# Winograd block sums of the down projection's data, made in the up projections instead of in the down projections

## The chip, the cores and the metric

One core of one Trainium2 chip. The metric is device time in microseconds of one execution; the kernel before takes 2208.18 us, the median of 3 runs (2207.48 to 2209.02).

## The reference

Two layers on a sequence of 1024 tokens of width 1024, float32. Layer 0 mixes tokens with a chunked gMLP, layer 1 with differential attention; each is followed by the gated MLP with a causal depthwise convolution, which is where the change lies. Around each sub-layer stand RMS norms and a residual.

```python
def conv_ffn(x, w_up, conv_w, conv_b, w_down):          # w_up: 1024 x 5632, w_down: 2816 x 1024
    h = causal_dwconv(x @ w_up, conv_w, conv_b)         # 3 taps
    g, u = h[..., :D_FF], h[..., D_FF:]                 # D_FF = 2816 = 22 x 128
    return (jax.nn.gelu(g) * u) @ w_down
...
    h = h + rmsnorm(y, norm_g[layer, 1])
    y = rmsnorm(h, norm_g[layer, 2])
    y = conv_ffn(y, ffn_w_up[layer], ffn_conv_w[layer], ffn_conv_b[layer], ffn_w_down[layer])
    h = h + rmsnorm(y, norm_g[layer, 3])
```

## The kernel before

**Precision.** Every float32 product is made of three passes of a reduced float type: `split` (line 168) rounds an operand on ScalarE (line 170, `hi`) and takes the rest on VectorE (line 173, `lo`); the passes are hi x hi, hi x lo, lo x hi. So each operand tile costs one ScalarE cast and one VectorE subtraction before TensorE (line 162) can use it.

**Seven products for eight.** Large products are cut into 2 x 2 blocks and made by Winograd's form of Strassen's scheme: seven block products, with sums of blocks of both operands before and of the results after.

**Up projections** (`ffn`, from line 1081): a loop over 22 features j of 128 columns, each with its gate and its value column block, so 22 pairs and in each 7 products of 12 matmuls. The weights of a pair are loaded on SyncE, GpSimd makes four sums of them (lines 983, 986, 987, 991), they are split; `Winograd.rest` (line 1060) runs the products and collects them on ScalarE (line 1025) and VectorE (line 1029). Then `convolve(j)` works on the pair's two columns: ScalarE scales one (line 1092), VectorE adds two taps (line 1094), the same for the other, ScalarE applies gelu (line 1098), VectorE multiplies (line 1099), and the product, 128 features x 1024 tokens, is stored on the DRAM tensor `pd` in two halves of 512 tokens (line 1101). From j = 4 on, GpSimd also makes block sums of the down projection's weights (`weight_sum`, lines 400 to 403, stored on `td` in line 405).

**Down projections** (`down`, line 421). The data operand A is 2816 features x 1024 tokens: A11 and A12 are the first half of the tokens with features 0 to 10 and 11 to 21, A21 and A22 the second half. `load` (line 432) brings a whole block, 11 features, into three tiles `t8` of 8 KB per partition; there are 15 such tiles in all. `combine` (line 444) makes the block sums in place on GpSimd: six instructions each (five of two features, 1024 elements, one of one), four sums: S1 = A21 + A22, S2 = S1 - A11, S3 = A22 - S2 (equal to A11 - A21), S4 = A12 - S2. `product` makes one block product of 132 matmuls: six pairs (k, n) of features; `operands` splits the data pair x and the weight pair w (raw weights in 4 tiles `wr`, split ones in 7 tiles `w4`); the last `tail` pairs are run row block by row block, so that results come out one by one. The order is A11 B11, A22 T4, A12 B21, S2 T2, S1 T1, S4 B22, S3 T3. For the results of the last two, `end` (line 328) adds norm and residual (lines 337, 343, 306 on VectorE) and stores.

**What sets the order.** The Tile layer puts the instructions of each engine into one in-order queue when the program is built, by its own model of when each can run, so an instruction may stand elsewhere than in the code. Every engine runs its queue in order; a waiting instruction holds all behind it. All DMAs stand on SyncE's queue, the loads into `wr` and `t8` among them, which wait there until a tile is free.

## Time and profile before

| | us |
|---|---|
| median of 3 runs (lowest, highest) | 2208.18 (2207.48, 2209.02) |
| profiled execution | 2211.13 |
| its span | 2209.4 |
| TensorE busy | 2132.1 (97%) |
| VectorE busy | 1697.2 (77%) |
| ScalarE busy | 1089.0 (49%) |
| GpSimd busy | 892.2 (40%) |

The mean granted clock of TensorE is 0.988 of full speed. In the profile PE is TensorE, PEld its weight loads, DVE VectorE, ACT ScalarE, POOL GpSimd, SPq SyncE's queue. A row names the line, the engine, the operation and the tiles that it writes and reads, without their numbers. The up projections run from about 340 to 760 us in layer 0 and from 1540 to 1980 in layer 1, each followed by a down projection to about 970 us and to the end. Busy shares over the whole span hide stages with different limits, so stretches are read one by one.

### The profile page before, as it was taken

Reading aid. Unit: us, or ns where it says so; the run is one execution under the profiler, and the core shown is the slowest. Engines: PE = TensorE matmul, PEld = TensorE weight load, DVE = VectorE, ACT = ScalarE, POOL = GpSimd, SP = SyncE. Lnnn points to the kernel's source line nnn. Section 1 sums busy time; section 2 is a strip of 40 time slices with the busy share of each in tenths; the row PEclk is TensorE's granted clock in tenths of the full one; section 3 lists DMA queues with packets and bytes.
Section 4 is the critical chain, followed back from the end, with each engine's and each line's share of the span. In section 5 each row is a group of like instructions: output and inputs, shape, how many; then the busy total and the mean of one; then the engine's idle time right before and its main releaser. Section 6 shows DMA issues by size and latency. Waiting matters only on the chain.

```text
span 2209.4 us, 27390 instructions
## 1 busy us (share of the span) xinstructions
PE 2132.1 (97%) x10072; PEld 1736.2 (79%) x10072; DVE 1697.2 (77%) x1967; ACT 1089.0 (49%) x1914; POOL 892.2 (40%) x751
## 2 busy tenths in 40 slices
PE   8979998999999998999999999999899999999998
PEld 6868786888888877887777777778688888887787
DVE  6654659878888788588588888866988888878856
ACT  5322435545455544465356665654545555554443
POOL 1264126666657084143000101222565666618512
PEclk9989999999999999999999999999999999999999
DMA  6232422544444562354411110233244444456224
GB/s 238 86 124 92 162 86 74 195 143 150 155 162 149 203 225 90 110 183 132 155 34 53 49 49 20 86 134 124 69 135 161 161 148 158 160 187 235 86 96 167
DMA packets 156647, 288.63 MB, mean 131 GB/s; under 512 B 11360, under 2 KB 75744, under 8 KB 156512
## 3 DMA queue, kind: packets, MB, share of 16 engines
q1 hardware_dynamic: 156512, 286.88, 37.9%
q8 instruction: 79, 1.29, 0.2%
q14 instruction: 56, 0.46, 0.1%
HBM read 210.29 MB, written 76.55 MB: 130 GB/s over the span
## 4 chain that ended last, share of the span: by engine, by line
PE 81%; DVE 10%; ACT 3%; DMA 2%; POOL 2%; issue 2%; SPq 0%; DVEq 0%; POOLq 0%; ACTq 0%
PE ps L162 77%; DVE t L173 2%; PE pst L162 2%; DVE w L173 2%; PE pst L843 1%; ACT e L824 1%; PE pst L296 1%; DVE t L1094 1%; DVE cols L1029 0%; DVE xs L306 0%; DVE e L830 0%; DMA wr<-in_b_wv 0%; DVE h L343 0%; DMA wr<-td 0%; DVE sm L821 0%
## 5 line engine op out<-in xcount | busy, mean ns | idle before, releaser
L162 PE MATMUL ps<-t,w 128*128 128x512 f32 x4848 | 1150.3, 394 | 16.2 <-ACT tm L1025 7.3
L162 PEld LDWEIGHTS ps<-t,w 128*128 128x128 f32 x4848 | 900.5, 189 | 215.6 <-ACT tm L1025 9.9
L162 PE MATMUL ps<-w,t 128*128 128x512 f32 x2512 | 602.4, 396 | 18.8 <-DVE t L173 12.6
L162 PEld LDWEIGHTS ps<-w,t 128*128 128x128 f32 x2512 | 472.7, 190 | 122.3 <-DVE t L173 16.5
L173 DVE TENSOR_TENSOR w<-wr,w 128x512 fp32r<-128x512 f32 (+1 forms) x266 | 334.4, 1263 | 160.8 <-ACT w L170 71.0
L170 ACT CAST w<-wr 128x512 fp32r<-128x512 f32 (+1 forms) x268 | 218.5, 821 | 212.7 <-PE ps L162 207.5
L1094 DVE SCALAR_TENSOR_TENSOR t<-cols,cw,t 128x1023 f32<-128x1023 f32 (+1 forms) x176 | 260.7, 1481 | 19.0 <-ACT t L1092 17.1
L173 DVE TENSOR_TENSOR t<-t,t 128x1024 fp32r<-128x1024 f32 (+1 forms) x124 | 185.2, 1525 | 16.2 <-ACT t L170 16.2
L446 POOL TENSOR_TENSOR t<-t,t 128x1024 f32<-128x1024 f32 (+1 forms) x48 | 147.2, 3103 | 115.9 <-PE ps L162 114.6
L173 DVE TENSOR_TENSOR w<-wt,w 128x512 fp32r<-128x512 f32 x176 | 169.6, 974 | 18.2 <-ACT w L170 18.1
L1025 ACT COPY tm<-ps 128x512 f32<-128x512 f32 x136 | 79.0, 581 | 150.8 <-PE ps L162 150.8
L170 ACT CAST t<-t 128x1024 fp32r<-128x1024 f32 (+1 forms) x124 | 105.6, 888 | 79.1 <-PE ps L162 57.8
L983 POOL TENSOR_TENSOR wt<-wr,wr 128x512 f32<-128x512 f32 x44 | 66.5, 1512 | 192.4 <-DMA wr<-in_ffn_up 128.5
L1092 ACT ACTIVATE t<-cols,cw 128x1024 f32<-128x1024 f32 x88 | 109.7, 1247 | 57.4 <-DVE cols L1029 57.2
L162 PE MATMUL ps<-t,t 64*128 64x512 f32 (+4 forms) x792 | 129.2, 376 | 0.8 <-ACT e L824 0.4
L202 POOL TENSOR_SCALAR sm<-sm 128x1 f32<-128x1 f32 (+1 forms) x48 | 15.4, 322 | 265.7 <-ACT ot L863 161.1
L338 POOL TENSOR_SCALAR sm<-sm 128x1 f32<-128x1 f32 x32 | 22.3, 698 | 245.0 <-ACT y L336 244.7
L170 ACT CAST w<-wt 128x512 fp32r<-128x512 f32 x176 | 108.2, 622 | 22.5 <-PE ps L162 15.5
L162 PEld LDWEIGHTS ps<-t,t 64*128 64x128 f32 (+1 forms) x792 | 91.2, 188 | 34.3 <-issue 11.1
L824 ACT ACTIVATE e<-ps,sm 128x128 f32<-128x128 f32 (+7 forms) x128 | 94.2, 745 | 28.8 <-DVE sm L816 22.7
L173 POOL TENSOR_TENSOR t<-wr,t 128x1024 fp32r<-128x1024 f32 (+1 forms) x16 | 36.4, 2281 | 171.1 <-ACT t L170 171.1
L1029 DVE TENSOR_TENSOR cols<-ps,tm 128x512 f32<-128x512 f32 x132 | 90.0, 682 | 18.1 <-PE ps L162 16.4
(155 smaller groups left out, 2453.4 us busy)
## 6 DMA issues: line engine op xcount, KB each, us to landing
wr<-in_ffn_up SPq DMA_DIRECT2D x88, 512.0 KB, 4.0
wr<-in_ffn_down SPq DMA_DIRECT2D x94, 256.0 KB, 3.4
pd<-t SPq DMA_DIRECT2D x88, 256.0 KB, 2.6
td<-wr SPq DMA_DIRECT2D x88, 256.0 KB, 2.5
wr<-td SPq DMA_DIRECT2D x40, 512.0 KB, 3.7
t<-pd SPq DMA_DIRECT2D x16, 1024.0 KB, 8.1
wr<-in_ffn_down SPq DMA_DIRECT2D x30, 512.0 KB, 3.6
hd<-h SPq DMA_DIRECT2D x24, 512.0 KB, 2.6
```

The lines of the kernel that those rows point to most:

```text
L162: nc.tensor.matmul(o, a, b, start=first, stop=last, skip_group_check=onto)
L170: i = nc.scalar.copy(hi, src)
L173: return (engine or nc.vector).tensor_tensor(lo, src, hi.bitcast(F32), ALU.subtract)
L296: nc.tensor.transpose(pt[:, k * P:(k + 1) * P], xs[:, f:f + P], ident)
L338: nc.gpsimd.tensor_scalar(ss, sq[:, 0:1], sq[:, 1:2], EPS, ALU.add, ALU.add)
L446: nc.gpsimd.tensor_tensor(of(o, k, n), of(a, k, n), of(b, k, n), op)
L824: nc.scalar.activation(e[:, :L], si[i], AF.Exp, bias=negm[:, i:i + 1], accum_out=sm[:, i:i + 1])
L983: i = nc.gpsimd.tensor_tensor(t1, b12, b11, ALU.subtract)
L1025: nc.scalar.copy(t, o)
L1029: nc.vector.tensor_tensor(o, a, b, ALU.add)
L1092: nc.scalar.activation(tt, src, AF.Identity, bias=c[:, 3:4], scale=c[:, 2:3])
L1094: nc.vector.scalar_tensor_tensor(tt[:, tap:], src[:, :S - tap], c[:, 2 - tap:3 - tap], tt[:, tap:], ALU.mult, ALU.add)
```

## The change

The features are taken in the order 0, 11, 1, 12, and so on (`feature`), so that an even and the following odd j hold feature k of A11, A21 and feature k of A12, A22. An even j multiplies into a tile `t8` that is kept until the odd one is done, and stores A11. An odd j stores A12 and A22; then GpSimd makes S3, S1, S2 and S4 of 512 elements each in the kept tile and each is stored. `pd` now holds seven blocks of 11 features. In `down`, `load`, `of` and `combine` are gone, and `operands` loads each data pair itself (line 432 after the change) into its own tile, 512 KB a load.

```diff
@@ -427,27 +427,10 @@
         nk = NFF // 2
         pairs = [(k, min(2, nk - k)) for k in range(0, nk, 2)]
         weights = weight_blocks(io["ffn_down"][l], td[l])
-        raw = {}
-
-        def load(a):
-            half, j = int(a[1]) - 1, (int(a[2]) - 1) * nk
-            raw[a] = []
-            for k in range(0, nk, 4):
-                n = min(4, nk - k)
-                t = t8(F32, (P, 4, 512))
-                nc.sync.dma_start(t[:, :n], pd[l][half, j + k:j + k + n].rearrange("j p c -> p j c"))
-                raw[a].append(t)
-
-        def of(a, k, n):
-            return raw[a][k // 4][:, k % 4:k % 4 + n]
-
-        def combine(o, a, b, op):
-            for k, n in pairs:
-                nc.gpsimd.tensor_tensor(of(o, k, n), of(a, k, n), of(b, k, n), op)
-
         def operands(a, b, k, n, apart=False):
-            x = t8(F32R, (P, 2, 2, 512))
-            split(x[:, 0, :n], x[:, 1, :n], of(a, k, n))
+            x, r = t8(F32R, (P, 2, 2, 512)), t8(F32, (P, 4, 512))[:, :n]
+            nc.sync.dma_start(r, pd[l][PARTS.index(a), k:k + n].rearrange("j p c -> p j c"))
+            split(x[:, 0, :n], x[:, 1, :n], r)
             raw = raw_w(weights[b](k, n).rearrange("k p c -> p k c"), n, 512)
             if apart:
                 t = t8(F32R, (P, 2, 2, 512))
@@ -457,7 +440,7 @@
             split(*w, raw)
             return x, w
 
-        def product(a, b, ahead=(), first=None, at=3, tail=SHORT_TAIL, wide=0):
+        def product(a, b, ahead=(), tail=SHORT_TAIL, wide=0):
 
             out = [bank1() for _ in range(4)]
 
@@ -473,8 +456,6 @@
                 xw = ahead[m] if m < len(ahead) else operands(a, b, k, n)
                 for i in range(4):
                     part(i, k, n, *xw)
-                if m == at and first:
-                    first()
             xws = [operands(a, b, k, n, m >= tail - wide) for m, (k, n) in enumerate(pairs[-tail:])]
             for i in range(4):
                 for (k, n), xw in zip(pairs[-tail:], xws):
@@ -482,42 +463,36 @@
                 yield i, out[i]
 
         add = nc.vector.tensor_tensor
-        load("A11")
         ahead = [operands("A11", "B11", *pairs[0])]
         yield
         with tc.tile_pool(name=nm("out"), bufs=1) as pool:
             u2, c11, v = (pool.tile([P, 4, 512], F32, tag=n, name=nm(n)) for n in ("u2", "c11", "v"))
-            for i, r in product("A11", "B11", ahead, lambda: load("A22")):
+            for i, r in product("A11", "B11", ahead):
                 nc.scalar.copy(u2[:, i], r)
             gp = load_g(pool, g_post)
             gn = load_g(pool, g_pre) if g_pre is not None else None
-            load("A21")
-            for i, r in product("A22", "T4", (), lambda: load("A12"), 1):
+            for i, r in product("A22", "T4"):
                 nc.scalar.copy(v[:, i], r)
-
-            combine("A21", "A21", "A22", ALU.add)
-            combine("A11", "A21", "A11", ALU.subtract)
-            combine("A22", "A22", "A11", ALU.subtract)
             for i, r in product("A12", "B21"):
                 add(c11[:, i], r, u2[:, i], ALU.add)
-            combine("A12", "A12", "A11", ALU.subtract)
-            for i, r in product("A11", "T2"):
+            for i, r in product("S2", "T2"):
                 add(u2[:, i], r, u2[:, i], ALU.add)
                 nc.gpsimd.tensor_tensor(v[:, i], v[:, i], u2[:, i], ALU.add)
             u4 = t8(F32, (P, 4, 512))
-            for i, r in product("A21", "T1"):
+            for i, r in product("S1", "T1"):
                 add(u4[:, i], r, u2[:, i], ALU.add)
-            for i, r in product("A12", "B22"):
+            for i, r in product("S4", "B22"):
                 c12 = pool.tile([P, 512], F32, tag="c12", name=nm("c12"), bufs=2)
                 add(c12, r, u4[:, i], ALU.add)
                 end(pool, i, (c11[:, i], c12), h_in, h_out, gp, gn, y_next, n=2)
-            for i, r in product("A22", "T3", tail=TAIL, wide=WIDE):
+            for i, r in product("S3", "T3", tail=TAIL, wide=WIDE):
                 add(v[:, i], r, v[:, i], ALU.add)
                 add(u4[:, i], r, u4[:, i], ALU.add)
                 end(pool, 4 + i, (v[:, i], u4[:, i]), h_in, h_out, gp, gn, y_next, n=2)
 
     hd = [dpool.tile([S, D], F32, name=f"hd{i}", tag=f"hd{i}") for i in range(3)]
-    pd = [dpool.tile([2, NFF, P, 512], F32, name=f"pd{i}", tag=f"pd{i}") for i in range(2)]
+    PARTS = ("A11", "A12", "A22", "S1", "S2", "S3", "S4")
+    pd = [dpool.tile([len(PARTS), NFF // 2, P, 512], F32, name=f"pd{i}", tag=f"pd{i}") for i in range(2)]
     td = [dpool.tile([2, NFF // 2, P, 2, 512], F32, name=f"td{i}", tag=f"td{i}") for i in range(2)]
     tv = dpool.tile([2, KT // 2, P, 2, 512], F32, name="tv", tag="tv")
     vd = dpool.tile([NT, P, D], F32, name="vd", tag="vd")
@@ -1080,13 +1055,20 @@
 
     def ffn(l, y, h_in, h_out, g_pre, y2):
         with tc.tile_pool(name=f"wg{l}", bufs=1) as wg, tc.tile_pool(name=f"ff{l}", bufs=1) as pool:
+            def feature(j):
+                return j // 2 + j % 2 * (NFF // 2)
+
             def pair(j):
-                return Winograd(wg, (io["ffn_up"][l, j], io["ffn_up"][l, NFF + j]), y, j < 2)
+                f = feature(j)
+                return Winograd(wg, (io["ffn_up"][l, f], io["ffn_up"][l, NFF + f]), y, j < 2)
+
+            first = []
 
             def convolve(j, cols):
+
                 ts = []
                 for gu in range(2):
-                    c = cw[:, gu * NFF + j, :]
+                    c = cw[:, gu * NFF + feature(j), :]
                     src = cols[gu]
                     tt = pool.tile([P, S], F32, tag="t", name=nm("t"), bufs=3)
                     nc.scalar.activation(tt, src, AF.Identity, bias=c[:, 3:4], scale=c[:, 2:3])
@@ -1096,9 +1078,28 @@
                         )
                     ts.append(tt)
                 nc.scalar.activation(ts[0], ts[0], AF.Gelu_apprx_tanh)
-                nc.vector.tensor_tensor(ts[0], ts[0], ts[1], ALU.mult)
-                for half in range(2):
-                    nc.sync.dma_start(pd[l][half, j], ts[0][:, half * 512:(half + 1) * 512])
+                store = lambda a, t: nc.sync.dma_start(pd[l][PARTS.index(a), j // 2], t)
+                if j % 2 == 0:
+                    first.append(t8(F32))
+                    a = first[-1][:, 0, :]
+                    nc.vector.tensor_tensor(a, ts[0], ts[1], ALU.mult)
+                    store("A11", a[:, :512])
+                else:
+                    nc.vector.tensor_tensor(ts[0], ts[0], ts[1], ALU.mult)
+                    f = first.pop().rearrange("p i (h c) -> p i h c", h=2)
+                    a11, a21, s2, s3 = f[:, 0, 0], f[:, 0, 1], f[:, 1, 0], f[:, 1, 1]
+                    a12, a22 = ts[0][:, :512], ts[0][:, 512:]
+                    store("A12", a12)
+                    store("A22", a22)
+                    add = nc.gpsimd.tensor_tensor
+                    add(s3, a11, a21, ALU.subtract)
+                    store("S3", s3)
+                    add(a21, a21, a22, ALU.add)
+                    store("S1", a21)
+                    add(s2, a21, a11, ALU.subtract)
+                    store("S2", s2)
+                    add(a11, a12, s2, ALU.subtract)
+                    store("S4", a11)
 
             sums = [[j - 4] if j >= 4 else [] for j in range(NFF)]
             for i, j in enumerate((8, 11, 14, 17)):
```

GpSimd in the middle of the up projections, layer 0. The names `wt` and `wr` are weight tiles, those of lines 958 to 966 (983 to 991 before) for the up projection and those of 400 to 403 for the down projection's sums; `t` are the kept tile and an odd feature's product. One pair before:

```order
L983 TENSOR_TENSOR wt_3771<-wr_3694,wr_3692 128x512
L400 TENSOR_TENSOR wr_3794<-wr_3794 128x256
L986 TENSOR_TENSOR wt_3772<-wr_3694,wt_3771 128x512
L401 TENSOR_TENSOR wr_3794<-wr_3794 128x256
L402 TENSOR_TENSOR wr_3794<-wr_3794 128x256
L403 TENSOR_TENSOR wr_3794<-wr_3794 128x256
L987 TENSOR_TENSOR wt_3774<-wr_3692,wt_3772 128x512
L991 TENSOR_TENSOR wt_3773<-wr_3694 128x512
```

One with an odd feature's sums after:

```order
L958 TENSOR_TENSOR wt_3642<-wr_3557,wr_3555 128x512
L400 TENSOR_TENSOR wr_3665<-wr_3665 128x256
L961 TENSOR_TENSOR wt_3643<-wr_3557,wt_3642 128x512
L401 TENSOR_TENSOR wr_3665<-wr_3665 128x256
L402 TENSOR_TENSOR wr_3665<-wr_3665 128x256
L403 TENSOR_TENSOR wr_3665<-wr_3665 128x256
L1097 TENSOR_TENSOR t_499_3164<-t_499_3164,t_3308 128x512
L962 TENSOR_TENSOR wt_3645<-wr_3555,wt_3643 128x512
L1099 TENSOR_TENSOR t_499_3164<-t_499_3164 128x512
L1101 TENSOR_TENSOR t_499_3164<-t_3308,t_499_3164 128x512
L966 TENSOR_TENSOR wt_3644<-wr_3557 128x512
```

Lines 1097, 1099 and 1101 (S1, S2, S4) now stand ahead of the pair's last weight sum, on line 966; S3 (line 1095) stands in the pair before.

VectorE at the end of the product S4 B22 in layer 0. `c` is the tile of its result (line 512 before, 486 after), `t` on line 173 are splits for the product S3 T3 that follows, from data or, read from `wr`, from weights. Before:

```order
L173 TENSOR_TENSOR t_1175_7415<-t_977_6213,t_1175_7415 128x1024
L173 TENSOR_TENSOR w_1135_7247<-wr_7244,w_1134_7246 128x512
L173 TENSOR_TENSOR t_1177_7420<-wr_7418,t_1177_7420 128x1024
L173 TENSOR_TENSOR t_1178_7423<-t_977_6213,t_1178_7423 128x1024
L173 TENSOR_TENSOR t_1180_7428<-wr_7426,t_1180_7428 128x1024
L173 TENSOR_TENSOR t_1181_7431<-t_978_6215,t_1181_7431 128x1024
L173 TENSOR_TENSOR t_1183_7436<-wr_7434,t_1183_7436 128x1024
L173 TENSOR_TENSOR w_1171_7380<-wr_7377,w_1170_7379 128x1024
L173 TENSOR_TENSOR t_1184_7439<-t_978_6215,t_1184_7439 128x512
L512 TENSOR_TENSOR c_1136_7259<-ps_1108_7096,t_1079_6901 128x512
L173 TENSOR_TENSOR t_1186_7444<-wr_7442,t_1186_7444 128x512
L337 TENSOR_TENSOR y_7263<-c_1136_7259,gb_6275 128x512
```

After, from the last of the four results on:

```order
L486 TENSOR_TENSOR c_1192_7461<-ps_1140_7199,t_1102_6989 128x512
L173 TENSOR_TENSOR t_1215_7538<-wr_7536,t_1215_7538 128x1024
L337 TENSOR_TENSOR y_7465<-c_967_6166,gb_6363 128x512
L337 TENSOR_TENSOR y_7465<-c_1192_7461,gb_6363 128x512
L173 TENSOR_TENSOR t_1216_7541<-t_1217_7542,t_1216_7541 128x1024
L173 TENSOR_TENSOR t_1219_7548<-wr_7546,t_1219_7548 128x1024
L343 SCALAR_TENSOR_TENSOR h_7436<-y_7435,sm_7434,h_7436 128x1024
L306 SCALAR_TENSOR_TENSOR xs_7416<-h_7406,sm_7417,gb_6365 128x1024
L173 TENSOR_TENSOR t_1220_7551<-t_1221_7552,t_1220_7551 128x1024
L173 TENSOR_TENSOR t_1223_7558<-wr_7556,t_1223_7558 128x1024
L173 TENSOR_TENSOR t_1224_7561<-t_1225_7562,t_1224_7561 128x512
L173 TENSOR_TENSOR t_1227_7568<-wr_7566,t_1227_7568 128x512
```

Before, the splits stand ahead of the first result, all but one; after, seven stand behind the fourth, with the norms of lines 337, 343 and 306 in between.

SyncE ahead of the product S4 B22, layer 0: `wr` are loads of weights, `t` loads of data. Before:

```order
L177 DMA wr_7103<-in_ffn_down 128x2x512
L177 DMA wr_7136<-in_ffn_down 128x2x512
L177 DMA wr_7169<-in_ffn_down 128x2x512
L177 DMA wr_7202<-in_ffn_down 128x2x512
L177 DMA wr_7235<-in_ffn_down 128x2x512
L177 DMA wr_7244<-in_ffn_down 128x512
L177 DMA wr_7377<-td_77 128x2x512
```

After:

```order
L177 DMA wr_7205<-in_ffn_down 128x2x512
L177 DMA wr_7240<-in_ffn_down 128x2x512
L177 DMA wr_7275<-in_ffn_down 128x2x512
L177 DMA wr_7310<-in_ffn_down 128x2x512
L177 DMA wr_7345<-in_ffn_down 128x2x512
L432 DMA t_1142_7201<-pd_75 128x2x512
L432 DMA t_1147_7236<-pd_75 128x2x512
L432 DMA t_1152_7271<-pd_75 128x2x512
L177 DMA wr_7356<-in_ffn_down 128x512
```

The first three loads of S4's data come behind five loads of weights.

## Rows read from the trace of the kernel before

**Rows 1.** The page's busy times: us, share of span, instructions

```profile
PE 2132.1 (97%) x10072; PEld 1736.2 (79%) x10072; DVE 1697.2 (77%) x1967; ACT 1089.0 (49%) x1914; POOL 892.2 (40%) x751
```

**Rows 2.** Stretches, up projections of layer 0; the first line names the columns

```profile
core 0: us, PE busy (x) PEld busy (x) DVE busy (x) ACT busy (x) POOL busy (x), PEclk, DMA share, GB/s
420.00:740.00 320.00, 319.88 (x1411) 264.75 (x1410) 267.07 (x255) 162.70 (x236) 191.86 (x144) 1.00 0.46 159
```

**Rows 3.** Stretches: down projections of layer 0, and (last) of layer 1

```profile
780.00:860.00 80.00, 71.73 (x292) 56.93 (x291) 77.46 (x31) 28.76 (x38) 72.62 (x24) 0.94 0.45 157
780.00:800.00 20.00, 17.83 (x79) 14.49 (x78) 19.81 (x7) 10.07 (x13) 20.00 (x7) 1.00 0.88 326
840.00:860.00 20.00, 15.22 (x56) 11.69 (x55) 18.19 (x12) 3.94 (x8) 12.62 (x5) 0.83 0.27 79
880.00:960.00 80.00, 80.00 (x355) 66.30 (x354) 53.56 (x57) 38.66 (x53) 18.53 (x16) 1.00 0.40 135
2000.00:2080.00 80.00, 70.60 (x292) 56.18 (x291) 76.42 (x31) 29.74 (x38) 73.52 (x24) 0.96 0.46 157
```

**Rows 4.** TensorE's waits, 760 to 870 us: total, times, longest

```profile
PE ps L162 <- DVE t L173: 5.3, 3, 3.9
PE ps L162 <- DVE w L173: 2.9, 2, 2.2
```

**Rows 5.** Line 446 by form: ns min/median/max, first and last start

```profile
L446 POOL TENSOR_TENSOR t<-t,t x48: 1726/3375/3478, 779.6 to 2072.0; 128x1024 f32<-128x1024 f32 x40, 128x512 f32<-128x512 f32 x8
```

**Rows 6.** Line 173 by form, data tiles, 780 to 850 us

```profile
L173 DVE TENSOR_TENSOR t<-t,t x12: 2822/3414/3428, 780.2 to 848.2; 128x1024 fp32r<-128x1024 f32 x10, 128x512 fp32r<-128x512 f32 x2
```

**Rows 7.** The same from 880 to 940 us

```profile
L173 DVE TENSOR_TENSOR t<-t,t x12: 679/1216/1226, 880.9 to 937.9; 128x1024 fp32r<-128x1024 f32 x10, 128x512 fp32r<-128x512 f32 x2
```

**Rows 8.** By line, 420 to 740 us: busy, mean, idle; then by form

```profile
L991 POOL TENSOR_TENSOR wt<-wr 128x512 f32<-128x512 f32 x16 | 28.7, 1794 | 0.0
...
L1094 DVE SCALAR_TENSOR_TENSOR t<-cols,cw,t 128x1023 f32<-128x1023 f32 x68 | 102.7, 1510 | 6.2 <-ACT t L1092 5.6
...
L1094 DVE SCALAR_TENSOR_TENSOR t<-cols,cw,t x68: 1267/1284/2349, 418.2 to 728.2; 128x1023 f32<-128x1023 f32 x34, 128x1022 f32<-128x1022 f32 x34
```

**Rows 9.** Timeline of ScalarE, feature 4: start, duration, instruction, idle before

```profile
441.37 0.57 ACT L1025 COPY tm<-ps 128x512 f32<-128x512 f32 x1
...
445.84 0.59 ACT L1025 COPY tm<-ps 128x512 f32<-128x512 f32 x1 [2.10 <-PE ps L162]
```

**Rows 10.** Timeline, feature 17: GpSimd, VectorE, TensorE's weight loads

```profile
...
683.98 1.74 POOL L987 TENSOR_TENSOR wt<-wr,wt 128x512 f32<-128x512 f32 x1
684.76 2.04 DVE L1094 SCALAR_TENSOR_TENSOR t<-cols,cw,t 128x1023 f32<-128x1023 f32 x1 [0.19 <-ACT t L1092]
...
685.68 2.28 POOL L991 TENSOR_TENSOR wt<-wr 128x512 f32<-128x512 f32 x1
...
687.33 1.71 DVE L1094 SCALAR_TENSOR_TENSOR t<-cols,cw,t 128x1022 f32<-128x1022 f32 x1
...
690.71 2.37 PEld L162 LDWEIGHTS ps<-t,w 128*128 128x128 f32 x11 [0.54 <-ACT tm L1025]
```

**Rows 11.** Timeline, feature 12's pair: GpSimd and the first gate tap

```profile
586.28 1.75 POOL L991 TENSOR_TENSOR wt<-wr 128x512 f32<-128x512 f32 x1
...
589.56 1.28 DVE L1094 SCALAR_TENSOR_TENSOR t<-cols,cw,t 128x1023 f32<-128x1023 f32 x1 [0.45 <-ACT t L1092]
...
590.91 0.74 POOL L400 TENSOR_TENSOR wr<-wr 128x256 f32<-128x256 f32 x1 [2.88 <-DMA wr<-in_ffn_down]
```

**Rows 12.** DMA issues: KB each, median us from issue to landing

```profile
pd<-t SPq DMA_DIRECT2D x88, 256.0 KB, 2.6
```

**Rows 13.** Timeline of VectorE, end of the last product but one

```profile
943.89 0.68 DVE L173 TENSOR_TENSOR t<-t,t 128x512 fp32r<-128x512 f32 x1
944.49 0.68 DVE L512 TENSOR_TENSOR c<-ps,t 128x512 f32<-128x512 f32 x1
...
947.50 1.28 DVE L343 SCALAR_TENSOR_TENSOR h<-y,sm,h 128x1024 f32<-128x1024 f32 x1 [0.25 <-POOL sm L339]
```

## The prediction

> **What bounds the kernel now.** I read the page's busy times first: TensorE is busy 97% of the span [rows 1], so 2132 us can't be beaten by moving other engines' work; what can be won is only where TensorE runs below its pace. Then I cut the span into stretches. In the up projections of layer 0 TensorE is full, 319.88 of 320 us, with VectorE at 267 and GpSimd at 192 [rows 2]. In the second half of a down projection it is full as well, 355 matmuls in 80 us. In between lie 80 us in each layer in which it does 292, VectorE is busy 77.46 and 76.42 us and GpSimd 72.62 and 73.52, and in the last 20 us the granted clock is 0.83 [rows 3]. There TensorE waits for splits on VectorE (line 173) five times, 8.2 us together, the longest 3.9 [rows 4]. The work beside them is `combine` on line 446: 48 GpSimd sums, 40 of them 1024 wide, median 3375 ns [rows 5]. While it runs, a split of a 1024-wide data tile takes a median of 3414 ns, with a smallest value, for the half-wide tile, of 2822 [rows 6]; in the 60 us after it the same group has a median of 1216 and a largest of 1226 [rows 7]. A pair of blocks needs two such splits while TensorE uses 24 matmuls, 24 x 80/355 = 5.4 us: 2 x 1.22 fits, 2 x 3.4 doesn't.
>
> **What the change removes.** All 24 sums in a layer's down projection. The splits fall back to 1.22 us, so VectorE needs 2.4 us in 5.4 there, and TensorE can run at the pace of the later stretch. Missing matmuls: 355 - 292 = 63 in each layer; at 80/355 = 0.225 us each that is 14.2 us, in both layers 28.4. This holds the waits (8.3 us of TensorE's idle time in layer 0, 80 - 71.73) and what the lower clock cost. It is the most that can be won: the number of matmuls stays.
>
> **What it adds in the up projections.** Per odd feature four 512-wide sums on GpSimd, 44 in a layer, 88 in all. The nearest row is line 991, a 512-wide subtraction from SBUF to SBUF in the same stage, 1794 ns in the mean [rows 8]: 44 x 1.79 = 79 us of GpSimd per layer, some 7.2 us in each 38 us of two pairs. GpSimd goes from 60% to about 79% busy there. VectorE is the question: it is at 83%, and each sum slows what runs beside it. The taps of the convolution (line 1094) show how much: 1267 ns the least and 1510 in the mean [rows 8]. Uncovered TensorE cost arises at one place. Two taps gate the gelu on ScalarE, and behind the gelu on ScalarE's in-order queue stands the copy of the next pair's second sum (line 1025), which TensorE's third product needs. With taps of 1.28 the copy ends at 441.94 and the next such copy, after 12 matmuls of that third product, starts at 445.84 [rows 9]: 3.90 us, of which 12 x 0.225 = 2.7 are matmuls and some 0.1 (an estimate) the way from one engine to the other, so 1.1 us is slack. In feature 17's pair lines 987 and 991 ran beside the two gate taps; they took 2.04 and 1.71 us, 1.2 us more than alone, and TensorE's weight load waited 0.54 us for the copy [rows 10]; of that the matmuls lost 0.12, all that is missing in the 320 us, since weight loads run ahead. So one meeting of both taps with GpSimd costs the whole slack and hardly more.
>
> In the kernel before GpSimd is mostly through when the gate taps come: at feature 12 line 991 ended at 588.03, the first tap ran at 589.56 in 1.28 us, and the next GpSimd work began at 590.91 [rows 11]. After the change three of the new sums of an odd feature stand ahead of the last subtraction, two of them between it and line 987 (now 966 and 962), and none can begin before that feature's product is made. So S2, S4 and the subtraction come 4 to 5 us later, on the gate taps of every even feature. That is 10 pairs in a layer, 20 in all. Bounds: nothing, where slack holds; and if both taps take the 2.28 us of line 991 [rows 10], 2 x 2.28 - 2.56 - 1.1 = 0.9 us each, 18 us. Nearest row: feature 17's, 0.1 for 1.2 us of delay; with a few pairs worse than that I take 0.3 us, 6 us in all.
>
> The Trainium skill bears on this (SBUF — State Buffer, section SBUF: two separate sides): an operation with two SBUF inputs on VectorE and one on GpSimd take the pair as a lock, and the loser waits for the other's whole instruction. The splits of rows 6 and 7 agree. By it the sums don't vanish but block VectorE elsewhere: 44 x 1.79 = 79 us per layer if every one met a VectorE operation at its start, and with 53 us idle in the 320 that would fill VectorE. The taps' mean, 0.24 us above the least, says that by far not each meeting costs a whole instruction; the sum goes by the rows.
>
> Stores of products rise from 88 of 256 KB [rows 12] to 7 per two features, 154, beside DMA engines at 0.46 in that stage [rows 2]; in the SyncE queue the stores of S1, S2 and S4, which wait for the sums, stand ahead of the next loads of up weights, so these go out some 4 us later in every other pair. GpSimd has 192 us in 16.8 pairs [rows 2], 11.4 a pair, and at most 5.4 more with three sums: 16.8 of 19.04 us. That still fits, so I cost it at nothing; if that cover is gone, TensorE waits for weight splits, and each microsecond past the period is one lost.
>
> **What it adds in the down projections.** Loads of 512 KB per pair of blocks in place of 1 MB loads four pairs ahead: 11 blocks of 256 KB of data and as many of weights, 5.8 MB per product of 132 matmuls (29.7 us), 194 GB/s against the 326 of one 20 us stretch [rows 3]. Bandwidth is no limit; order is. The SyncE queue puts five weight loads, each waiting for one of four raw tiles, ahead of the first data of S4, so a data tile that could be loaded long before comes only when weight splits have freed their tiles. In the last product the splits of pairs 2 to 5 now stand behind the sums and norms of S4's result: before, all of them but one stood ahead of the first sum, which ran at 944.49 with the norms behind it [rows 13]. After, seven (five of 1.22, two of 0.68) stand behind the last of the four sums, with two norm operations of 1.28 [rows 13] and two half-wide ones, taken at 0.68, among them: 7.5 + 2.6 + 1.4 = 11.5 us; TensorE has 24 matmuls of the first pair and 27 of the first row's rest, 11.5 us, to cover that, but it needs the middle splits before the last ones. I judge it just enough or late by 1 to 3 us. Bounds for a layer: 0, and 7 (late at both places, 3 us each, and 1 for clock). I take 2 per layer, 4 us.
>
> **The sum.** 2211.13 (the profiled execution; span 2209.4) - 28.4 + 6 + 4 = 2192.7. The three timed runs' median is 2208.18, 2.95 below the profiled one, so 2189.8 us for the median: 0.8% faster.
>
> **The rivals.**
> A. *Nothing is given back.* The new sums find gaps and the loads are early. For it: slack of 1.1 us in most pairs, loads bound by nothing. Against: the sums' place on the gate taps. 2211.13 - 28.4 - 2.95 = 2179.8.
> B. *The down projections wait for their own loads.* Data behind weights in one queue, splits behind the norms: 7 us in each layer in place of 2. 2189.8 + 10 = 2199.8. For it: the order of VectorE and SyncE; against: four raw tiles and the data tiles free early in a product at 1.22 us per split.
> C. *The up projections pay 0.9 us at each even feature*, 18 instead of 6: 2201.8. For it: the lock between the engines; against: only feature 17's pair of layer 0 shows any loss.
> D. *Slower: VectorE becomes the bound of the up projections.* It has 53 us free in 320, 3.2 per pair, much of it waiting for ScalarE's casts and not free to be used. If each new sum blocks VectorE for its own 1.79 us, an odd pair and the next need 2 x 15.9 + 7.2 = 39.0 us in 38.1, and TensorE waits for the taps at every even feature. It decides from 28.4/20 = 1.4 us of stall per even feature on; at 0.9 + 0.9 from the overfull pair it costs 36 us: 2211.13 - 28.4 + 36 + 4 - 2.95 = 2219.8. For it: 3.4 us splits in `combine`'s stretch; against: the taps' mean. The rule of the Trainium skill named above (SBUF — State Buffer) would make this case.
>
> **How the numbers follow.** My forecast 0.50, own range 2184 to 2197; A 0.13; B 0.12; C 0.12; D 0.13. 0.2% is 4.4 us, about what a measurement here can tell from no change: faster means below 2203.8. Forecast and A are faster, B and C by two thirds: 0.50 + 0.13 + 0.16 = 0.79, which I lower to 0.75, since unseen waits can add to each; same 0.12; slower 0.13. The range 2179 to 2210 leaves out D and a little below A.
>
> **What would show it.** Right: no matmul gap and clock 1.00 in the stretches of the first three products, splits of 1.22 us there; in the up stage VectorE up by 20 to 45 us per layer, taps of even features at 1.7 to 2.3 us, and short waits of TensorE for line 1025. Down: waits for `t` splits at the start of S4 and S3. Wrong: TensorE waits above 1 us at most even features (D), or weight splits late because GpSimd is (line 961 to 966), or product starts that wait on `t<-pd` loads.

## The result: 4.3% slower, where 0.8% faster was forecast

The changed kernel takes 2302.88 us (median of 4 runs, 2301.24 to 2304.65) against 2208.6 for the kernel before (4 runs): ratio 1.0427, 95% interval 1.0411 to 1.0444. The gain in the down projections came as forecast; the up projections lost more than four times as much.

The page's busy times of the changed kernel, for [rows 1]:

```profile
PE 2151.8 (94%) x10072; PEld 1738.9 (76%) x10072; DVE 1649.7 (72%) x1967; ACT 1083.3 (47%) x1914; POOL 908.6 (40%) x791
```

Its stretches (time, then busy us and instructions of each engine, granted clock, DMA share, GB/s): the up projections of layer 0 for [rows 2], then 80 us of the down projection of either layer where before stood `combine` [rows 3]:

```profile
420.00:740.00 320.00, 274.55 (x1164) 220.31 (x1163) 226.24 (x208) 129.34 (x194) 216.53 (x154) 0.96 0.41 142
820.00:900.00 80.00, 80.00 (x355) 66.24 (x354) 48.06 (x42) 40.05 (x46) 6.44 (x3) 1.00 0.75 260
2100.00:2180.00 80.00, 80.00 (x355) 66.24 (x354) 48.27 (x46) 43.41 (x53) 0.00 (x0) 1.00 0.76 266
```

Down, TensorE does 355 matmuls in 80 us instead of 292. Both traces hold the same 1788 matmuls of an up stage, and from the last of them to the end of the down projection's last long run of matmuls it takes 204.5 us in either layer before and 192.1 after: 24.9 us won in both together. Up, it does 1164 instead of 1411 in 320 us, and neither VectorE (71%) nor GpSimd (68%) is full. From the first of those 1788 matmuls to the last it takes 482.0 instead of 418.7 us in layer 0 and 466.0 instead of 415.4 in layer 1: 114 us lost.

The splits of data tiles in the down projection, 820 to 900 us, as in [rows 6] and [rows 7], and the taps as in [rows 8] (ns min/median/max):

```profile
L173 DVE TENSOR_TENSOR t<-t,t x21: 685/1225/2315, 819.3 to 899.3; 128x1024 fp32r<-128x1024 f32 x18, 128x512 fp32r<-128x512 f32 x3
...
L1076 DVE SCALAR_TENSOR_TENSOR t<-cols,cw,t x56: 1268/1740/2418, 420.2 to 722.3; 128x1023 f32<-128x1023 f32 x28, 128x1022 f32<-128x1022 f32 x28
```

The splits fell from 3414 to 1225 ns; the taps' median rose from 1284 to 1740.

TensorE's largest waits in the whole kernel (total, times, longest), the same two in the kernel before, then ScalarE's after the change from 420 to 740 us:

```profile
PE ps L162 <- ACT tm L1000: 56.4, 27, 6.4
PE ps L162 <- DVE cols L1004: 37.1, 13, 6.0
```

```profile
PE ps L162 <- ACT tm L1025: 7.3, 4, 2.5
...
PE ps L162 <- DVE cols L1029: 0.2, 1, 0.2
```

```profile
ACT w L170 <- POOL wt L966: 74.4, 14, 7.5
ACT w L170 <- DMA wr<-in_ffn_up: 26.9, 11, 5.2
```

So 86 of the 114 us are these two waits; the rest went with slower matmuls, for the granted clock is 0.96 in the stretch where it was 1.00 [rows 2]. Neither of ScalarE's two waits is among those of the kernel before in that stretch. TensorE waits for the copy (line 1000, 1025 before) as the prediction said, but mostly not because of taps: 21 of its 26 waits above 0.3 us, 47 of the 56 us, come within 16 us of a cast that was held for the pair's last weight sum, seven of them with taps of 1.27 to 1.29 us. The longest round shows how it comes about; rows of ScalarE, GpSimd, the gate taps and TensorE, with GpSimd's wait for raw weights and the sum S3 (line 1095) first:

```profile
512.63 2.29 POOL L958 TENSOR_TENSOR wt<-wr,wr 128x512 f32<-128x512 f32 x1 [6.35 <-DMA wr<-in_ffn_up]
...
518.21 2.27 POOL L1095 TENSOR_TENSOR t<-t 128x512 f32<-128x512 f32 x1
...
523.54 1.28 POOL L966 TENSOR_TENSOR wt<-wr 128x512 f32<-128x512 f32 x1
524.85 0.62 ACT L170 CAST w<-wt 128x512 fp32r<-128x512 f32 x1 [6.92 <-POOL wt L966]
...
526.90 0.59 ACT L1050 COPY cols<-ps 128x512 f32<-128x512 f32 x1
...
529.83 0.62 ACT L170 CAST w<-wr 128x512 fp32r<-128x512 f32 x1 [2.34 <-DMA wr<-in_ffn_up]
530.36 1.24 ACT L1074 ACTIVATE t<-cols,cw 128x1024 f32<-128x1024 f32 x1
...
531.63 1.98 DVE L1076 SCALAR_TENSOR_TENSOR t<-cols,cw,t 128x1023 f32<-128x1023 f32 x1 [0.45 <-ACT t L1074]
532.50 1.70 POOL L400 TENSOR_TENSOR wr<-wr 128x256 f32<-128x256 f32 x1
...
534.14 2.37 DVE L1076 SCALAR_TENSOR_TENSOR t<-cols,cw,t 128x1022 f32<-128x1022 f32 x1
...
536.60 1.06 ACT L1080 ACTIVATE t<-t 128x1024 f32<-128x1024 f32 x1 [1.11 <-DVE t L1076]
...
537.56 0.57 ACT L1000 COPY tm<-ps 128x512 f32<-128x512 f32 x1
...
538.18 1.22 PE L162 MATMUL ps<-t,w 128*128 128x512 f32 x2 [6.43 <-ACT tm L1000]
```

GpSimd gets the pair's raw weights at 512.6 and works without a pause; the pair's last weight sum (line 966) ends at 524.8, late. The cast of it has held ScalarE for 6.92 us; then come the copies, a cast that waits 2.34 for a weight load, and the scaling of the convolution only at 530.36. The taps take 1.98 and 2.37 us beside GpSimd, then gelu, the copy, and TensorE, which has waited 6.43 us.

The other wait, for `cols` on VectorE (line 1004), goes through the kept tile. The even product (line 1085) waits for the stores of the sums that were made in the tile, and behind it on VectorE stands the sum that TensorE needs:

```profile
736.80 1.23 DVE L1085 TENSOR_TENSOR t<-t,t 128x1024 f32<-128x1024 f32 x1 [8.76 <-DMA pd<-t]
...
738.54 0.68 DVE L1004 TENSOR_TENSOR cols<-ps,tm 128x512 f32<-128x512 f32 x1
...
739.28 6.01 PE L162 MATMUL ps<-t,w 128*128 128x512 f32 x18 [5.96 <-DVE cols L1004]
```

All twelve of these waits above 0.3 us stand right behind such a wait of the even product, of 4.7 to 8.8 us.

### The profile page after: what moved, and what is told of

Same layout as the page of the kernel before. It is cut to its first block, busy times and chain, and to the rows that moved or that the text cites. A ratio compares the mean times of both kernels' runs of the same rounds, so it can differ in the third digit from the quotient of the medians.

```text
span 2299.4 us, 27706 instructions
## 1 busy us (share of the span) xinstructions
PE 2151.8 (94%) x10072; PEld 1738.9 (76%) x10072; DVE 1649.7 (72%) x1967; ACT 1083.3 (47%) x1914; POOL 908.6 (40%) x791
## 3 DMA queue, kind: packets, MB, share of 16 engines
q8 instruction: 79, 1.29, 0.2%
## 5 line engine op out<-in xcount | busy, mean ns | idle before, releaser
L162 PE MATMUL ps<-t,w 128*128 128x512 f32 x4848 | 1180.4, 400 | 100.8 <-ACT tm L1000 56.4
L162 PEld LDWEIGHTS ps<-t,w 128*128 128x128 f32 x4848 | 909.9, 191 | 321.3 <-ACT tm L1000 70.7
L162 PE MATMUL ps<-w,t 128*128 128x512 f32 x2512 | 592.1, 392 | 2.0 <-DVE t L173 1.1
L173 DVE TENSOR_TENSOR w<-wr,w 128x512 fp32r<-128x512 f32 (+1 forms) x266 | 282.3, 1067 | 143.0 <-PE ps L162 75.6
L1076 DVE SCALAR_TENSOR_TENSOR t<-cols,cw,t 128x1023 f32<-128x1023 f32 (+1 forms) x176 | 293.5, 1667 | 15.6 <-ACT t L1074 9.6
L173 DVE TENSOR_TENSOR w<-wt,w 128x512 fp32r<-128x512 f32 x176 | 179.8, 1037 | 43.1 <-ACT w L170 43.1
L170 ACT CAST w<-wt 128x512 fp32r<-128x512 f32 x176 | 105.3, 621 | 204.5 <-POOL wt L966 163.3
L173 DVE TENSOR_TENSOR t<-t,t 128x1024 fp32r<-128x1024 f32 (+1 forms) x124 | 139.5, 1145 | 78.5 <-ACT t L170 77.0
L1085 DVE TENSOR_TENSOR t<-t,t 128x1024 f32<-128x1024 f32 x22 | 27.5, 1248 | 100.6 <-DMA pd<-t 100.6
L480 POOL TENSOR_TENSOR v<-v,u 128x512 f32<-128x512 f32 x8 | 12.0, 1498 | 203.8 <-issue 197.3
```

The lines of the kernel that those rows point to most:

```text
L162: nc.tensor.matmul(o, a, b, start=first, stop=last, skip_group_check=onto)
L170: i = nc.scalar.copy(hi, src)
L173: return (engine or nc.vector).tensor_tensor(lo, src, hi.bitcast(F32), ALU.subtract)
L480: nc.gpsimd.tensor_tensor(v[:, i], v[:, i], u2[:, i], ALU.add)
L1076: nc.vector.scalar_tensor_tensor(tt[:, tap:], src[:, :S - tap], c[:, 2 - tap:3 - tap], tt[:, tap:], ALU.mult, ALU.add)
L1085: nc.vector.tensor_tensor(a, ts[0], ts[1], ALU.mult)
```

## The experiments

All medians come from runs beside the kernel before on the same chip; the ratio has its 95% interval. The expectations weigh five theories: (1) the one kept tile closes a loop; (2) stores that wait for sums hold up the weight loads on SyncE; (3) GpSimd and VectorE block each other; (4) the sums lengthen GpSimd's round of a pair, and the late last weight sum holds up ScalarE; (5) VectorE's and GpSimd's operations on SBUF share one budget of time per pair.

**First guess: one kept tile.** In the changed kernel the even product (line 1085) waits 100.6 us in all for stores out of the kept tile:

```profile
DVE t L1085 <- DMA pd<-t: 100.6, 15, 8.8
```

*Two kept tiles*, and the same layout with one (S2 and S1 then overwrite A11 and A21, S3 and S4 get places of their own):

```diff
-    expo = base.tile([P, 112], F32, tag="expo", name="expo")[:, :8]
+    expo = base.tile([P, 8], F32, tag="expo", name="expo")
...
-                    first.append(t8(F32))
-                    a = first[-1][:, 0, :]
+                    a = [hold[:, 0], own][j // 2 % 2]      # two_tiles; one_tile: hold[:, 0]
+                    first.append(a)
...
```

> Edit: even products go in turn into two tiles of 4 KB (one half of a t8 tile and a new one), so that a product no longer waits for the stores of the sums two features earlier; S2 in place of A11, S1 in place of A21, S3 and S4 in the other half of the t8 tile. Same sums, same stores. Theory 1 (one kept tile closes a loop: the even product waits on VectorE for the last stores of the pair before, the weight splits behind it free raw tiles late, GpSimd gets its weights late, the sums and their stores come late): the 100 us of waits of the even product for stores are gone, time 2188 to 2205. Theory 2 (stores that wait for sums stand ahead of the weight loads on SyncE): 2280 to 2305, GpSimd still waits for weight loads. Theory 3 (GpSimd and VectorE block each other, the rival D of the prediction): 2280 to 2305.

> Edit: the same layout as with two tiles, but every even product goes into the same 4 KB half. Theory 1: 2285 to 2310 as in the changed kernel, with 80 to 110 us of waits of the even product for stores; theories 2 and 3: also 2280 to 2305, that is, the same as with two tiles.

Measured: two tiles 2357.4 us, 1.0675 (1.0656 to 1.0695); one tile 2344.83, 1.0617 (1.0596 to 1.0639). With two tiles that wait is gone from VectorE, and TensorE waits for the copy all the more:

```profile
PE ps L162 <- ACT tm L1000: 98.8, 34, 6.9
```

Theory 1 fell: in the same layout the run without that wait is 13 us slower than the one with it (73.7 us of it there), so the wait of the product was a symptom. Both times lie outside every range. They can't be held against the changed kernel, because the first lines of the edit change more than the kept tile: in these two runs the stages before and behind the up projections are slower too, the first ones among them, where the code is the same. From the start to 300 us, the changed kernel and then one tile (ns min/median/max); below them the down projection with one tile, to be read beside 355 matmuls in 80 us:

```profile
L162 PE MATMUL ps<-w,t x523: 387/389/795, 10.6 to 299.8; 128*128 128x512 f32 x175
L162 PE MATMUL ps<-w,t x516: 390/397/796, 10.6 to 299.4; 128*128 128x512 f32 x172
```

```profile
840.00:920.00 80.00, 80.00 (x343) 64.33 (x342) 43.27 (x39) 37.35 (x43) 7.01 (x3) 1.00 0.72 248
```

With one tile TensorE is 3% slower at a granted clock of 1.00. At 80/343 - 80/355 = 0.008 us each, the 3576 matmuls of the two up stages alone make 28 us, and the up stages are 22 us longer than in the changed kernel; the other 17 of the 39 us between the two traces lie outside them. So the pace by itself is enough for the 42 us between the medians. Why the narrower `expo` goes with slower matmuls isn't shown.

**The sums alone, and the change without sums.**

```diff
...
+                if j % 2:        # sums_alone: kernel before, f is a t8 tile that nothing reads
+                    sub(f[:, 0, 0], a, b, ALU.subtract)
+                    sub(f[:, 0, 1], a, b, ALU.add)
+                    sub(f[:, 1, 0], f[:, 0, 1], a, ALU.subtract)
+                    sub(f[:, 1, 1], a, f[:, 1, 0], ALU.subtract)
```

> The kernel before plus four 512-wide GpSimd sums after every odd feature, into a tile that nothing reads and nothing stores; combine stays. It gives the price of the added GpSimd work alone. Theory 1: 2208 to 2222. Theory 2: 2208 to 2222, since no store waits for them. Theory 3: 2300 to 2330, since the gain of the down projections (27 us) is missing.

```diff
-                    add(s3, a11, a21, ALU.subtract)
-                    store("S3", s3)
+                    store("S3", a11)     # no_sums: S1, S2 and S4 likewise
```

> The changed kernel without its GpSimd sums: the seven blocks are stored and loaded as before, but S1 to S4 hold plain blocks, so the result is another one. One kept tile, all stores and loads stay. Theory 1: 2180 to 2195, as the stores wait for nothing and land early. Theories 2 and 3: the same. If it stays above 2250, the stores' number or the new order of the features is the cause, and no theory holds.

Measured: 2277.69 us, 1.0313 (1.0296 to 1.0329), and 2277.76 in one more run of the same edit; without sums 2197.99, 0.9953 (0.9936 to 0.9969). The first lies between the ranges of theories 1 and 2 and of theory 3, the second 3 us above its own. So 88 sums that nothing waits for cost 68 us, and leaving them out of the change gives 105 us back. The stretch 420 to 740 us with the sums alone, and one of the sums there (ns min/median/max):

```profile
420.00:740.00 320.00, 298.10 (x1268) 242.87 (x1267) 277.34 (x229) 142.39 (x211) 259.22 (x172) 0.97 0.42 141
```

```profile
L1110 POOL TENSOR_TENSOR t<-t,t x9: 1292/1742/2283, 444.2 to 769.0; 128x512 f32<-128x512 f32 x9
```

VectorE's busy time per pair of 84 matmuls is 277.34 x 84/1268 = 18.4 us, against 267.07 x 84/1411 = 15.9 before, with the same instructions. In the changed kernel itself, where VectorE often waits, it is 226.24 x 84/1164 = 16.3.

**The sums on VectorE.** `add = nc.vector.tensor_tensor` in place of `nc.gpsimd.tensor_tensor` in `convolve`.

> Edit: the changed kernel with the four sums on VectorE (nc.vector in place of nc.gpsimd), some 0.7 to 0.8 us each, 44 a layer. Theory 4 (the sums lengthen GpSimd's round of a pair: wait for the weight load, four weight sums, sums for the down weights, over the 19 us of TensorE's pair; the cast that waits for the last weight sum holds ScalarE and with it the copy of TensorE's result): the waits of ScalarE's casts for the last weight sum go back to a few us and the time is 2185 to 2205, near the one without sums. Theory 3 (VectorE and GpSimd block each other): also faster than the changed kernel, 2190 to 2215. If VectorE itself were full: 2230 to 2260.

Measured: 2215.03 us, 1.0028 (1.0016 to 1.0041): 88 us better than on GpSimd, 17 worse than without sums, 10 above theory 4's range and at the upper end of theory 3's. The wait that theory 4 is about is all but gone, 2.0 us in place of 74.4 from 420 to 740 us:

```profile
ACT w L170 <- POOL wt L966: 2.0, 1, 2.0
```

**GpSimd kept busy without reading.** Memsets in place of the sums, in the kernel before:

```diff
...
+                    nc.gpsimd.tensor_scalar(f[:, 0:1], ts[0][:, 0:1], 1.0, 0.0, ALU.mult, ALU.add)
+                    for _ in range(4):
+                        nc.gpsimd.memset(f[:, :1270], 0.0)                # sets_alone
...
+                    for n in range(4):
+                        c = f[:, 512 * n:512 * n + 512]
+                        nc.gpsimd.tensor_scalar(c[:, 0:1], ts[0][:, 0:1], 1.0, 0.0, ALU.mult, ALU.add)
+                        for _ in range(2):
+                            nc.gpsimd.memset(c, 0.0)     # sets_ahead; sets_as_long: 3 x c[:, :448]
```

> The kernel before plus, after every odd feature, one 1-element GpSimd operation on its product and four GpSimd memsets of 1270 elements (about 1.3 us each, from 0.52 us for 512) into a tile that nothing reads: GpSimd is occupied about as long as by the four sums, but reads nothing from SBUF that could block VectorE; two of the memsets come to stand behind the last weight sum. Theory 3: 2203 to 2216, as before. Theory 4: 2225 to 2285, since only the time on GpSimd counts; the sums alone gave 2278.

> The kernel before plus, after every odd feature, four 1-element GpSimd operations on its product and eight GpSimd memsets of 512 elements (0.52 us each; 4.2 us of memsets, some 2 us of the small ones), all of them ahead of the pair's last two weight sums in GpSimd's queue, where the four sums alone stood. Theory 4 (time on GpSimd ahead of the last weight sum makes the weights late): 2240 to 2280, near the 2278 of the sums alone. Theory 5 (operations of GpSimd that read SBUF and VectorE's operations with two SBUF inputs hold each other up): 2205 to 2222, as with the memsets of which half stood behind the last weight sum.

> As sets_ahead, with twelve memsets of 448 elements (0.46 us each, 5.5 us) and the four small operations (1.9 us): 7.4 us of GpSimd per odd feature, all ahead of the last two weight sums, which is what the four sums alone took while VectorE worked beside them (4 x 1.85 us). Theory 4 (only the time on GpSimd counts): 2268 to 2285, as with the sums. Theory 5 (the sums also hold up VectorE): 2240 to 2262, a rest of 16 us or more to the sums' 2278.

Measured: 2217.28 us, 1.0043 (1.0025 to 1.0061), where half of the memsets stood behind the pair's last weight sum; 2239.65, 1.0152 (1.0131 to 1.0172), with all of them ahead of it; 2254.46, 1.0201 (1.0175 to 1.0226), with more of them ahead of it. By the traces the added work takes 5.3 us of GpSimd per odd feature in `sets_ahead` and 6.4 in `sets_as_long`, where 6.2 and 7.4 were expected; the four sums alone took 7.1, and with their least durations they would take 5.2. The first time lies 1 us above theory 3's range, the second 0.4 us below theory 4's, the third inside theory 5's. The memsets of the last, its stretch, and ScalarE's wait there:

```profile
L1110 POOL MEMSET t<- x108: 463/472/488, 436.2 to 761.6; 128x448 f32 x108
```

```profile
420.00:740.00 320.00, 305.29 (x1312) 249.42 (x1312) 260.30 (x234) 148.39 (x219) 259.49 (x269) 0.98 0.42 143
```

```profile
ACT w L170 <- POOL wt L991: 43.3, 6, 11.4
```

GpSimd is as busy in this stretch as with the sums (259.49 and 259.22 us), though with more matmuls done. VectorE needs 260.30 x 84/1312 = 16.7 us per pair, not 18.4, and no memset was stretched, while the sums were, from 1292 up to 2283 ns. So of the 68 us that the sums cost alone, at least some 45 go with GpSimd's time ahead of the last weight sums. The other 23 (2277.7 - 2254.5) aren't all VectorE's: the step from 5.3 to 6.4 us of memsets cost 15, so the 0.7 us by which the sums are longer may be worth some 9 (an estimate). Seen from the other side, sums of 5.2 us, not stretched, would hold GpSimd no longer than the memsets of `sets_ahead`, which cost 30; so some 38 of the 68 us (an estimate) arise because GpSimd and VectorE hold each other up, in part by stretching the sums. Theory 4 and theory 5 both have a share. Whether TensorE's copy would come in time if it stood ahead of the waiting cast in ScalarE's queue was not tested.

**Raw tiles.** The down weights' sums take a raw tile of their own pool, `pool.tile(..., tag="wa", bufs=1)` in line 392; `expo` is 8 columns wide here too.

> Edit: the raw tile of the down weights' sums (lines 392 to 405) comes from a pool of its own instead of sharing the four raw tiles with the up weights, so the up weights of a whole pair more can be loaded ahead. GpSimd does the same sums. Theory 4: the wait of GpSimd for the weight loads goes and most of the loss with it, 2195 to 2250. Theory 3: 2290 to 2310, no change to the changed kernel.

Measured: 2357.81 us, 1.0666 (1.0647 to 1.0685). Both ranges missed, and the total says little of the up weights' loads, because this run shares the slower matmuls (602 in 140 us below, a pace of 344 in 80). But the queue now has all down weight sums of layer 0 before 630 us, and the rest of the stage runs without them. Two stretches of the same kernel, first with weight sums, then without:

```profile
500.00:640.00 140.00, 113.22 (x452) 88.51 (x450) 79.41 (x79) 51.13 (x79) 93.39 (x79) 0.90 0.51 167
660.00:800.00 140.00, 140.00 (x602) 112.39 (x601) 110.07 (x108) 68.05 (x100) 75.46 (x45) 1.00 0.30 102
```

In the second, the new sums run as in the first, each at least three times, and TensorE doesn't stop.

**Without the weight sums**, lines 400 to 403 left out, all else as in the changed kernel:

> The changed kernel without the GpSimd sums of the down weights (lines 400 to 403; their loads and stores stay, so T1 to T4 hold plain blocks and the result is another one). The four new sums, their stores and the kept tile stay. Theory 5 (a budget that VectorE and GpSimd share: the least durations of VectorE's operations with two SBUF inputs and of GpSimd's sums add up to 19.6 us per pair before, 2.6 more after; TensorE's pair takes 19.04): without the 3.5 us of weight sums it is 18.7 and the loss goes, 2180 to 2205. Theory 2 (stores that wait for sums hold up the weight loads on SyncE): 2230 to 2300, since all of that stays.

Measured: 2176.43 us, 0.9854 (0.9836 to 0.9872). Theory 2 fell, and theory 5's range was missed by 4 us. Some 13 us of it come from before the up projections, where such sums stood too (the up stage starts at 318.9 us instead of 332.4). The up stages take 416.7 and 416.6 us, against 418.7 and 415.4 before the change. The stretch 420 to 740 us:

```profile
420.00:740.00 320.00, 319.32 (x1409) 264.05 (x1408) 262.47 (x250) 163.60 (x236) 159.38 (x94) 1.00 0.52 171
```

The sums, their stores, the kept tile and the new order of features cost nothing once GpSimd has room. The stores of the down weights no longer wait for sums in this run, so their raw tiles come free earlier as well; the two weren't separated.

**Stores that don't wait for sums.** S1 to S4 stored from plain blocks at once; the sums go into a tile that nothing reads.

> The changed kernel, but the blocks S1 to S4 are stored from plain blocks right away (so the result is another one) and the four GpSimd sums are made of A12 and A22 into the other half of the kept tile, which nothing stores: the sums are there and nothing waits for them, no store, no weight load. Theory 5: 2235 to 2265, that is the 2198 without sums plus the loss that the sums alone made in the kernel before (68), or somewhat less. Theory 2: 2195 to 2215.

Measured: 2283.83 us, 1.0335 (1.0319 to 1.0351). Above what theory 5 allowed, far above theory 2. Sums beside the change's own stores cost 2283.8 - 2198.0 = 86 us, and the changed kernel is 19 us slower still. Neither is a clean price, for something did wait: the sums went into the kept tile, and the next even product waited for them.

```profile
DVE t L1085 <- POOL t L1102: 69.2, 13, 6.9
```

**A better version.** The kernel before, `combine` on VectorE:

```diff
-                nc.gpsimd.tensor_tensor(of(o, k, n), of(a, k, n), of(b, k, n), op)
+                nc.vector.tensor_tensor(of(o, k, n), of(a, k, n), of(b, k, n), op)
```

> The kernel before with one edit: combine (line 446) runs on VectorE instead of GpSimd. 24 sums of 1.22 us and less are 28 us of VectorE in a layer, beside splits that take 1.22 instead of 3.4 us as nothing contends; the up projections stay as before. Theory 5: it wins most of the 27 us that the change won in the down projections and loses nothing above, 2183 to 2200, better than both kernels. If VectorE gets too full in the product A22 T4, where 18 of the sums stand: 2200 to 2212.

Measured: 2183.52 us, 0.9882 (0.9866 to 0.9899): 25 us faster than the kernel before, 119 faster than the changed one, at the low end of theory 5's range. Its two stretches of `combine` and the sums themselves (ns min/median/max):

```profile
780.00:860.00 80.00, 79.64 (x352) 65.61 (x350) 67.75 (x66) 38.26 (x47) 0.00 (x0) 1.00 0.51 173
2000.00:2080.00 80.00, 80.00 (x354) 66.24 (x354) 60.94 (x62) 36.42 (x44) 3.05 (x3) 1.00 0.35 115
```

```profile
L446 DVE TENSOR_TENSOR t<-t,t x48: 680/1219/1226, 779.3 to 2038.6; 128x1024 f32<-128x1024 f32 x40, 128x512 f32<-128x512 f32 x8
```

The same 48 sums take 1219 ns on VectorE instead of 3375 on GpSimd [rows 5]; VectorE does 66 instructions in the first stretch, sums among them, in less busy time than 31 took before (67.75 against 77.46 us).

## Why the prediction was wrong

- **The removal, -28.4 us, and the new waits of the down projections, +4 us:** right, in mechanism and size. Together they forecast 24.4 us won, and 24.9 were measured, with a clock of 1.00 and 355 matmuls in 80 us as in the later stretch. TensorE's waits in the down projections after the change are 1.4 us in layer 0, half of it still for the last copy of the up stage, and 2.4 in layer 1; those for splits come in the products S4 and S3, as it said. Rival B is out.
- **The up projections, +6 us:** the step that failed; 114 measured. Two sentences of it did. "That still fits, so I cost it at nothing" compared GpSimd's busy time, 16.8 us, with the 19.04 of a pair. But GpSimd also waits for each pair's raw weights, and the sums stand ahead of the pair's last weight sum, so what counts is when line 966 ends. From 420 to 740 us GpSimd stands idle 80.4 us ahead of a pair's first weight sum and is late all the same:

```profile
L958 POOL TENSOR_TENSOR wt<-wr,wr 128x512 f32<-128x512 f32 x13 | 20.7, 1589 | 80.4 <-DVE w L173 34.5 <-DMA wr<-in_ffn_up 33.4 <-DVE t L1076 12.4
```

  The price named there for a lost cover ("TensorE waits for weight splits") had the right origin, late weight sums, and no size and no chance; and TensorE hardly waits for those splits (8.6 us in the whole kernel, 15.5 before). And "uncovered TensorE cost arises at one place": the gate taps did get slower (median 1740), but the larger wait reached the same copy by another way, through a cast ahead of it in ScalarE's queue. A second place was not in the prediction at all: the even product that waits for the kept tile's stores, and behind it 37.1 us of TensorE's waits for `cols`.
- **The rate of contention:** the mean of the taps was read as "not each meeting costs a whole instruction" and the meetings elsewhere at nothing. The sums alone raise VectorE's busy time by 2.5 us per pair and stretch themselves from 1.29 to 1.74 us in the median.
- **Rival D** had the sign and a part of the cause (engines that block each other), a third of the price (36), and the wrong end: VectorE was not full but waiting.
- The rule of the Trainium skill (SBUF — State Buffer, section SBUF: two separate sides) is a lock held for a whole instruction. That agrees with sums that stretch and memsets that don't read and don't stretch. Taken to the letter it goes a little too far: the least durations of both engines' operations of that kind already add up to some 19.6 us per pair before the change (4 taps of 1.27, a product of 1.21, 7 splits of 0.67; 4 weight sums of 1.28 and 4 to 5 of 0.73), in a pair of 19.04 in which TensorE never stopped. That is 3% over, and the rows don't tell whether an operation holds the lock for all of its recorded duration. As an index of how close the stage stood to its limit the sum would have been a warning; that it is the limit is argued, not shown.

Left open: the 14 us by which the change without sums stays above 2208.8 - 24.9 = 2184, of which 7 lie in the up projections (422.5 and 418.8 us); and what the two waits of TensorE would each cost without the other.

## What to carry to other kernels

Work moved off a stage that waits isn't free in a stage that doesn't: add up what the receiving engine does there together with the engines it contends with, and look at which instruction stands last in its queue for whom, not at its busy share. When an engine makes another slow, try the slow one for the work first: one word put the sums on VectorE, where 1.2 us replaced 3.4 and both engines were relieved. And a wait that grows large in the profile may be a symptom; test it by taking it away before building on it. When an experiment also moves tiles about, compare a stage whose code is the same in both kernels first: here that would have told the slower matmuls from the effect of the edit.

## What was not expected of the hardware

GpSimd's memsets beside a VectorE at 81% kept 463 to 488 ns, while sums of two SBUF operands on GpSimd took 1292 to 2283 ns beside a VectorE at 87%. In the down projections a GpSimd sum of 1024 elements and a VectorE split each took some 3.4 us when both ran. On VectorE either took 1.22 us while GpSimd did no such sums: running the two side by side was slower than one after the other on one engine.

In all three runs with the narrower `expo` TensorE does 343 matmuls in 80 full us of a down projection instead of 355, at the same granted clock of 1.00. What it is in the placement of the tiles that does it, no run here shows.
